# Split projection weights kept in DRAM by the first token group and loaded by the others

## The chip, the cores and the metric

One of the eight cores of a Trainium2 chip runs the whole kernel. Its time is device time in microseconds of one execution, from the start of the program to its end. An execution's profile shows the span from the first to the last instruction; the execution itself lasts a little longer than that span.

## The reference

The reference is one inference step of one layer of a streaming encoder, for a prompt of 2048 tokens and a sample of 32 tokens, each of width 1024, all in float32:

```python
z = rmsnorm(x, norm_mix_g) @ w_in                       # 1024 -> 2560: q, k, v and the RWKV inputs
a_out = window_attention(q, k, v, ...)                  # 8 heads, 2 KV heads, window of 2 chunks of 64, sinks
r_out, shift, S = rwkv7_mixer(zr, ...)                  # 8 heads of 64, a recurrence over the tokens
x = x + concat(a_out, r_out) @ w_out                    # 1024 -> 1024
x = x + memory_cross_attention(rmsnorm(x), mem_k, mem_v) # 4 heads of 128, 256 memory tokens, w_cq and w_co
x = x + square(relu(rmsnorm(x) @ w_up)) @ w_down        # 1024 -> 4096 -> 1024
y = rmsnorm(x, norm_final_g)
```

It returns the two outputs y, and the key, value, shift and recurrence states.

## The kernel before, in words

Features lie on the 128 partitions, tokens along the free dimension. The 2080 tokens are cut into four groups: `GROUPS` has 544 tokens in group 0 (the sample first) and 512 in each of groups 1, 2 and 3. A group is projected in two halves of 272 or 256 tokens.

**Products in three parts.** A float32 weight is split into a high part `w_h`, in the rounded format that TensorE multiplies fast, and a low part `w_l`, the rest. Activations are split in the same way into `xh` and `xl`. `mm3` multiplies `w_h` by `xh`, `w_h` by `xl` and `w_l` by `xh` into one PSUM tile (lines 234, 235 and 236). So 24 matmuls make one block of 128 output features for one half of a group.

**Where the weights are split.** `load_w` (line 257 issues the load) works in two halves of 512 columns. For each it loads a raw tile of 256 KB over the SP queue, rounds it to `w_h` with an activation on ScalarE (through `split`, line 66), and subtracts that from the raw tile to get `w_l` on POOL or VectorE (line 69). There are `RB = 2` raw tiles and `WB = 2` pairs of `w_h` and `w_l`, which all dense layers of the first stage share. A pair is 1024 columns of high and as many of low parts: 0.5 MB each.

**Dense layers.** `dense` goes through the units of a weight matrix, one `load_w` for each, and multiplies each unit by both halves of the group. The input projection has 20 units (`win`), the output projection 8 (`wout`), the query projection of the cross-attention 4 (`wcq`), its output projection 4 of two blocks each (`wco`), and the memory's keys and values 4 each. A unit is loaded and split again for every group: 4 x 20 for `win` and 4 x 8 for `wout`. Nearly all `w_l` of this stage are made on POOL; the first two units of group 0 on VectorE (`fast`).

**Evacuation.** `evac` scales a block out of PSUM into `zo` (three tiles) on VectorE, mixes neighbouring tokens for the RWKV part, and stores it to DRAM over SP. `ophase` adds the residual `xres`.

**The phases.** `Y` and `Z` project a group's RWKV and attention inputs (`zphase`), `R` is one RWKV tile of 128 tokens, `A` one attention tile, `O` the output projection (`ophase`), `C`, `X` and `D` the cross-attention. A string `PLAN` fixes the order in which they are traced; `Y0` comes first, `Z0` after it, then the memory phase `M` and the phases of groups 1 to 3 interleaved with the RWKV and attention tiles. The RWKV tiles are a chain: each needs the state of the one before. Inside a tile, a triangular solve sends a matrix through DRAM (`lscr`, `lt`), runs 15 steps of two short VectorE operations each (`prd`, `xt`), and sends the result through DRAM again (`xscr`, `td`). After all this the MLP runs for six blocks of 352 or 320 tokens (`ps_up`, `ps_dn`), with weights split in the same way.

**What sets the order on each engine.** The instructions are traced with priorities (`setp`), and a planner that simulates the engines' times orders all instructions of each engine and queue at compile time. On the chip, each engine and each queue then runs its own list strictly in that order, and an instruction that waits holds back everything behind it on the same engine or queue. Nearly all loads and stores are issued by SP, a few stores by ScalarE. Tiles with the same tag rotate through their buffers; a new tile waits until all users of the old one are done.

Of the kernel before, what the change touches and what calls it, by code (L numbers as in the profile page):

```python
# [10 lines left out]
F32 = mybir.dt.float32  # L11
F32R = mybir.dt.float32r
# [5 lines left out]
P = 128  # L18
# [4 lines left out]
KC = D // P  # L23
# [13 lines left out]
TCKW = dict(schedule_with_timeline_sim=True)  # L37
E1, E2, E3, E4, E6, E7, E8 = "GGGVGGV"
PSOL, PSER, RB, SNB = "s", "s", 2, 3
XB, WB, XS = 5, 2, 4  # L40
BKB, ABB, TMB = 2, 2, 2

PG = dict(mix=0, cross=8, mlp=16, fin=24, mem=32, mu=40, w0=54, a0=58, kk=62, ka=66,
# [7 lines left out]
def hymba_step_kernel(  # L51
# [9 lines left out]
    V, G, S, T, Q = nc.vector, nc.gpsimd, nc.scalar, nc.tensor, nc.sync  # L61
# [15 lines left out]
    dram = ctx.enter_context(tc.tile_pool(name="dram", bufs=1, space=DRAM))  # L77
# [170 lines left out]
    zp = stage1.enter_context(tc.tile_pool(name="zp", bufs=1))  # L248
# [3 lines left out]
    def load_w(pool, src, n=1024, bufs=3, tag="w", eng=None, rb=RB, raw=None):  # L252
        wh = pool.tile([P, n], F32R, tag=tag + "h", name="w_h", bufs=bufs)
        wl = pool.tile([P, n], F32R, tag=tag + "l", name="w_l", bufs=bufs)
        for i in range(0, n, 512):
            w = (raw or pool).tile([P, 512], F32, tag="wraw", name="w_raw", bufs=rb)
            Q.dma_start(w, src[:, i:i + 512])
            split(w, wh[:, i:i + 512], wl[:, i:i + 512], ENG[E7] if eng is G and i else eng)
        return wh, wl
# [36 lines left out]
            gsplit(xk(k), xh[a][:, b, 0:nb], xl[a][:, b, 0:nb], pc(gkey, k))  # L296
        return xh, xl, lambda: rms(zp, xk, nb, "zt", pe, 3)

    def dense(wsrc, units, xs, blks, evac, nk=KC, per=1, rs=None, fast=False):
        cols = nk * P  # L300
        if rs is None:
            rs = [None] * len(blks)
        for u in units:
            wh, wl = load_w(zp, wsrc[u], bufs=WB, eng=V if fast and u < units[0] + 2 else G)
            for j in range(per):
                ft = u * per + j
                for bi, (b0, nb) in enumerate(blks):
                    if callable(xs[bi]):
                        xs[bi] = xs[bi]()
                    xh, xl, r = xs[bi]  # L310
                    ps = pmm("ps_z")
                    mm3(ps[:, 0:nb], lambda k: wh[:, j * cols + k * P:j * cols + (k + 1) * P],
                        lambda k: wl[:, j * cols + k * P:j * cols + (k + 1) * P],
                        lambda k: xh[k // XS][:, k % XS, 0:nb], lambda k: xl[k // XS][:, k % XS, 0:nb], nk)
                    if rs[bi] is None and r is not None:
                        rs[bi] = r()
                    evac(ft, bi, b0, nb, ps, rs[bi])
# [3 lines left out]
    def zphase(g, units):  # L321
        lab(f"Z{g}.prep")
        o, n = GROUPS[g]
        blks = halves_of(g)
# [5 lines left out]
        xs, rs = zst[g]  # L330
# [29 lines left out]
                    V.tensor_copy(carry[:, f:f + 1], zms[f])  # L360
            Q.dma_start(zqkv[g][:, ft, b0:b0 + nb] if ft < 6 else zrw[g][:, ft - 6, b0:b0 + nb], zo[:, 0:nb])

        dense(win, units, xs, blks, evac, rs=rs, fast=(g == 0 and 0 not in units))
        if 0 in units:
            zouts(g)
        else:
# [40 lines left out]
    def ophase(g):  # L407
        lab(f"O{g}")
        o, n = GROUPS[g]
        blks = halves_of(g)  # L410
        xs = [prep(mscr[g][:, :, b0:b0 + nb], nb, None) for b0, nb in blks]

        def evac(m, bi, b0, nb, ps, r):
            xr = zp.tile([P, NH], F32, tag="zm", name="xres", bufs=3)
            Q.dma_start(xr[:, 0:nb], xT3[:, m, o + b0:o + b0 + nb])
            zo = zp.tile([P, NH], F32, tag="zo", name="zo2", bufs=3)
            tt(zo[:, 0:nb], ps[:, 0:nb], xr[:, 0:nb], ADD)
            Q.dma_start(x2scr[g][:, m, b0:b0 + nb], zo[:, 0:nb])

        dense(wout, range(8), xs, blks, evac)  # L420

    def cqphase(g):
        lab(f"C{g}")
# [477 lines left out]
    xs, hhs, hls, vrs = {}, {}, {}, {}  # L901
# [26 lines left out]
    for it in PLAN.split():  # L928
# [6 lines left out]
        elif k in "RA":  # L935
            g = it[1] if it[1] == "s" else int(it[1])
# [104 lines left out]
    for s_ in range(start[5] + 16):  # L1041
        up = []
        for i in range(2):
            u = (2 * s_ + i) % 3
# [127 lines left out]
```

## Time and profile before

| | |
|---|---|
| median of three runs (lowest, highest) | 3261.2 us (3257.07, 3262.8) |
| the profiled execution | 3264.61 us |
| its span | 3262.8 us |
| mean granted TensorE clock | 0.960 |
| busy: TensorE, VectorE, ScalarE, POOL | 93%, 58%, 38%, 31% of the span |
| moved by DMA | 328.95 MB, mean 101 GB/s |

A busy share is the time in which an engine has an instruction under way, over the span; matmuls are pipelined, so a busy TensorE is not always at its peak rate. Of two operations with the same name, one belongs to a line of the kernel (L66 is an activation, L69 and L72 two forms of elementwise operation, all in helpers), so tile names tell them apart: `w_l<-w_raw,w_h` writes `w_l` and reads `w_raw` and `w_h`. "Idle before" is the time in which the engine stood still ahead of an instruction, put down to what ended it. The chain that ended last is followed back from the last instruction: at each step to what released it.

### The profile page before, as it was taken

How to read it: one execution, taken by the hardware profiler on the slowest of the kernel's cores; microseconds unless marked ns; L12 is line 12 of the kernel's file. 1: busy time of each engine (PE TensorE's matmuls, PEld its weight loads, DVE VectorE, ACT ScalarE, POOL GpSimd, SP SyncE). 2: the span in 40 equal slices, each digit the busy share in tenths (PEclk: the TensorE clock that was granted, in tenths of full speed). 3: DMA queues.
4: the chain of work that ended last, by engine and by line, in shares of the span. 5: the costliest groups of instructions: out<-in, count | busy, mean ns of one | idle time of the engine just before them, and what ended most of it. 6: DMA issues, size and time to landing. Idle time of an engine off the chain costs nothing.

```text
span 3262.8 us, 64716 instructions
## 1 busy us (share of the span) xinstructions
PE 3037.4 (93%) x25605; PEld 2850.0 (87%) x25605; DVE 1896.0 (58%) x4482; ACT 1247.0 (38%) x2824; POOL 1012.4 (31%) x1017
## 2 busy tenths in 40 slices
PE   8989888998879988898978999999999999999998
PEld 7877776877768977778978999999999999999998
DVE  4588777887777567853334544444445644444446
ACT  5355454444455444445443322222224322222223
POOL 3443354323354343425554410111013511011111
PEclk9989888999989999999989999999999999999999
DMA  5443343334344454446765211111113111111112
GB/s 167 134 115 108 104 130 108 108 96 122 109 122 123 135 150 120 130 129 195 242 214 178 68 51 41 46 46 52 40 46 115 66 44 52 40 52 52 46 46 91
DMA packets 336752, 328.95 MB, mean 101 GB/s; under 512 B 82320, under 2 KB 256064, under 8 KB 336448
## 3 DMA queue, kind: packets, MB, share of 16 engines
q1 hardware_dynamic: 306640, 311.83, 31.0%
q10 hardware_dynamic: 29808, 12.98, 1.6%
q8 instruction: 201, 3.29, 0.4%
q14 instruction: 103, 0.84, 0.1%
HBM read 252.59 MB, written 72.39 MB: 100 GB/s over the span
## 4 chain that ended last, share of the span: by engine, by line
PE 53%; DMA 8%; DVE 7%; ACT 3%; POOL 2%; issue 2%; SPq 1%; DVEq 0%; ACTq 0%; POOLq 0%
PE ps_up L236 7%; PE ps_dn L1002 7%; PE ps_dn L1004 7%; PE ps_dn L1003 7%; PE ps_up L234 7%; PE ps_up L235 7%; PE ps_z L234 2%; PE ps_z L236 2%; PE ps_z L235 2%; DMA xb<-x2scr 2%; DMA lt<-lscr 1%; ACT xh L66 1%; DVE z L69 1%; DVE prd L69 1%; DVE xt L69 1%
## 5 line engine op out<-in xcount | busy, mean ns | idle before, releaser
L234 PE MATMUL ps_z<-xh,w_h 128*128 128x256 f32 (+1 forms) x2368 | 722.8, 305 | 98.3 <-DVE zo L69 41.1
L236 PE MATMUL ps_z<-xh,w_l 128*128 128x256 f32 (+1 forms) x2368 | 715.0, 302 | 0.8 <-POOL w_l L69 0.8
L235 PE MATMUL ps_z<-xl,w_h 128*128 128x256 f32 (+1 forms) x2368 | 714.0, 302 | 1.4 <-DVE xl L72 0.8
L66 ACT ACTIVATE w_h<-w_raw 128x512 fp32r<-128x512 f32 x576 | 344.5, 626 | 777.7 <-PE ps_up L235 258.5
L69 DVE TENSOR_TENSOR x<-ps_dn,x 128x352 f32<-128x352 f32 (+1 forms) x768 | 389.6, 516 | 365.0 <-PE ps_dn L1004 364.5
L234 PEld LDWEIGHTS ps_z<-xh,w_h 128*128 128x128 f32 x2368 | 478.0, 202 | 124.1 <-DVE zo L69 34.2
L69 POOL TENSOR_TENSOR w_l<-w_raw,w_h 128x512 fp32r<-128x512 f32 x300 | 394.9, 1332 | 580.6 <-ACT w_h L66 481.0
L69 POOL TENSOR_TENSOR rl<-rl 128x352 f32<-128x352 f32 (+1 forms) x192 | 161.1, 840 | 1138.4 <-ACT uh L66 1136.4
L1002 PE MATMUL ps_dn<-uh,w_h 128*128 128x352 f32 (+1 forms) x1536 | 492.9, 321 | 4.2 <-DVE x L69 3.1
L236 PE MATMUL ps_up<-fh,w_l 128*128 128x352 f32 (+1 forms) x1536 | 495.4, 323 | 1.2 <-DVE w_l L69 1.2
L1003 PE MATMUL ps_dn<-ul,w_h 128*128 128x352 f32 (+1 forms) x1536 | 491.1, 320 | 5.0 <-DVE ul L69 5.0
L234 PE MATMUL ps_up<-fh,w_h 128*128 128x352 f32 (+1 forms) x1536 | 493.2, 321 | 0.5 <-DVE zo L69 0.5
L235 PEld LDWEIGHTS ps_z<-xl,w_h 128*128 128x128 f32 x2368 | 478.3, 202 | 15.9 <-issue 9.6
L236 PEld LDWEIGHTS ps_z<-xh,w_l 128*128 128x128 f32 x2368 | 478.0, 202 | 15.2 <-issue 10.4
L235 PE MATMUL ps_up<-fl,w_h 128*128 128x352 f32 (+1 forms) x1536 | 491.1, 320 | 0.1
L1004 PE MATMUL ps_dn<-uh,w_l 128*128 128x352 f32 (+1 forms) x1536 | 490.8, 320 | 0.0
L69 DVE TENSOR_TENSOR w_l<-w_raw,w_h 128x512 fp32r<-128x512 f32 x276 | 197.7, 735 | 222.0 <-ACT w_h L66 221.5
L1003 PEld LDWEIGHTS ps_dn<-ul,w_h 128*128 128x128 f32 x1536 | 289.9, 189 | 5.6 <-DVE ul L69 5.3
L1002 PEld LDWEIGHTS ps_dn<-uh,w_h 128*128 128x128 f32 x1536 | 288.6, 188 | 6.5 <-DVE x L69 3.0
L236 PEld LDWEIGHTS ps_up<-fh,w_l 128*128 128x128 f32 x1536 | 288.4, 188 | 1.7 <-DVE w_l L69 1.5
L1004 PEld LDWEIGHTS ps_dn<-uh,w_l 128*128 128x128 f32 x1536 | 289.2, 188 | 0.2
L234 PEld LDWEIGHTS ps_up<-fh,w_h 128*128 128x128 f32 x1536 | 288.3, 188 | 1.3 <-DVE zo L69 0.7
(245 smaller groups left out, 4478.5 us busy)
## 6 DMA issues: line engine op xcount, KB each, us to landing
w_raw<-in_win SPq DMA_DIRECT2D x160, 256.0 KB, 2.9
w_raw<-in_wup SPq DMA_DIRECT2D x136, 256.0 KB, 2.6
w_raw<-in_wdn SPq DMA_DIRECT2D x136, 256.0 KB, 2.6
w_raw<-in_wout SPq DMA_DIRECT2D x64, 256.0 KB, 3.2
zrw<-zo SPq DMA_DIRECT2D x84, 128.0 KB, 2.1
lt<-lscr SPq DMA_DIRECT2D x34, 244.0 KB, 3.8
zin<-zrw SPq DMA_DIRECT2D x16, 512.0 KB, 3.8
w_raw<-in_wcq SPq DMA_DIRECT2D x32, 256.0 KB, 3.4
```

Of the source, the lines that this page charges most:

```text
L66: S.activation(out, in_, func, **kw)
L69: (eng or V).tensor_tensor(out, a, b, op=op)
L234: T.matmul(ps, lhsT=a, rhs=c, start=(k == 0), stop=False)
L235: T.matmul(ps, lhsT=a, rhs=d, start=False, stop=False)
L236: T.matmul(ps, lhsT=b, rhs=c, start=False, stop=(k == nk - 1))
L1002: T.matmul(ps[:, 0:n], lhsT=wh[:, ms], rhs=us[i][0], start=(i == 0), stop=False)
L1003: T.matmul(ps[:, 0:n], lhsT=wh[:, ms], rhs=us[i][1], start=False, stop=False)
L1004: T.matmul(ps[:, 0:n], lhsT=wl[:, ms], rhs=us[i][0], start=False, stop=(i == 1))
```

## The change

`stage_w` takes the place of `load_w` in `dense`. For `win` and `wout` (`keep` is "in" or "out"), group 0 loads and splits each unit as before and then stores the finished `w_h` and `w_l` to two DRAM tiles, over SP. When groups 1, 2 and 3 come to the same unit, they load `w_h` and `w_l` from there, over SP, each in one transfer of 512 KB, straight into a pair of buffers; no raw tile, no activation and no subtraction is needed. `wcq`, `wco` and the memory's weights are split in place as before. The pairs of buffers become three (`WB = 3`) for all dense layers of the first stage.

```diff
--- before.py
+++ after.py
@@ -37,7 +37,7 @@
 TCKW = dict(schedule_with_timeline_sim=True)
 E1, E2, E3, E4, E6, E7, E8 = "GGGVGGV"
 PSOL, PSER, RB, SNB = "s", "s", 2, 3
-XB, WB, XS = 5, 2, 4
+XB, WB, XS = 5, 3, 4
 BKB, ABB, TMB = 2, 2, 2
 
 PG = dict(mix=0, cross=8, mlp=16, fin=24, mem=32, mu=40, w0=54, a0=58, kk=62, ka=66,
@@ -296,12 +296,31 @@
             gsplit(xk(k), xh[a][:, b, 0:nb], xl[a][:, b, 0:nb], pc(gkey, k))
         return xh, xl, lambda: rms(zp, xk, nb, "zt", pe, 3)
 
-    def dense(wsrc, units, xs, blks, evac, nk=KC, per=1, rs=None, fast=False):
+    wsaved = {}
+
+    def stage_w(wsrc, u, keep, fast):
+        key = (keep, u)
+        if key in wsaved:
+            dh, dl = wsaved[key]
+            wh = zp.tile([P, 1024], F32R, tag="wh", name="w_h", bufs=WB)
+            wl = zp.tile([P, 1024], F32R, tag="wl", name="w_l", bufs=WB)
+            Q.dma_start(wh.bitcast(F32), dh)
+            Q.dma_start(wl.bitcast(F32), dl)
+            return wh, wl
+        wh, wl = load_w(zp, wsrc[u], bufs=WB, eng=V if fast else G)
+        if keep is not None:
+            dh, dl = [dram.tile([P, 1024], F32, name=f"w{keep}{u}{c}") for c in "hl"]
+            Q.dma_start(dh, wh.bitcast(F32))
+            Q.dma_start(dl, wl.bitcast(F32))
+            wsaved[key] = (dh, dl)
+        return wh, wl
+
+    def dense(wsrc, units, xs, blks, evac, nk=KC, per=1, rs=None, fast=False, keep=None):
         cols = nk * P
         if rs is None:
             rs = [None] * len(blks)
         for u in units:
-            wh, wl = load_w(zp, wsrc[u], bufs=WB, eng=V if fast and u < units[0] + 2 else G)
+            wh, wl = stage_w(wsrc, u, keep, fast and u < units[0] + 2)
             for j in range(per):
                 ft = u * per + j
                 for bi, (b0, nb) in enumerate(blks):
@@ -360,7 +379,7 @@
                     V.tensor_copy(carry[:, f:f + 1], zms[f])
             Q.dma_start(zqkv[g][:, ft, b0:b0 + nb] if ft < 6 else zrw[g][:, ft - 6, b0:b0 + nb], zo[:, 0:nb])
 
-        dense(win, units, xs, blks, evac, rs=rs, fast=(g == 0 and 0 not in units))
+        dense(win, units, xs, blks, evac, rs=rs, fast=(g == 0 and 0 not in units), keep="in")
         if 0 in units:
             zouts(g)
         else:
@@ -417,7 +436,7 @@
             tt(zo[:, 0:nb], ps[:, 0:nb], xr[:, 0:nb], ADD)
             Q.dma_start(x2scr[g][:, m, b0:b0 + nb], zo[:, 0:nb])
 
-        dense(wout, range(8), xs, blks, evac)
+        dense(wout, range(8), xs, blks, evac, keep="out")
 
     def cqphase(g):
         lab(f"C{g}")
```

## Rows read from the trace of the kernel before

**Rows 1.** windows: length; PE, PEld, DVE, ACT, POOL busy; clock, DMA share, GB/s

```profile
0.00:118.00 118.00, 104.79 (x745) 98.05 (x746) 56.41 (x182) 57.49 (x128) 44.51 (x48) 1.00 0.50 161
118.00:170.00 52.00, 45.76 (x340) 42.67 (x338) 32.02 (x53) 20.12 (x39) 25.57 (x21) 0.93 0.44 134
170.00:1500.00 1330.00, 1177.22 (x13478) 1015.06 (x13478) 984.85 (x2699) 660.73 (x1590) 531.63 (x498) 0.92 0.42 120
1500.00:1770.00 270.00, 236.09 (x1793) 228.61 (x1793) 84.79 (x191) 123.92 (x294) 132.10 (x139) 0.93 0.70 224
1770.00:3262.00 1492.00, 1473.56 (x9257) 1465.66 (x9255) 737.90 (x1360) 384.76 (x774) 278.55 (x311) 1.00 0.17 55
```

**Rows 2.** the page's chain that ended last, share of the span by engine

```profile
PE 53%; DMA 8%; DVE 7%; ACT 3%; POOL 2%; issue 2%; SPq 1%; DVEq 0%; ACTq 0%; POOLq 0%
```

**Rows 3.** the chain from 800 to 1770 us, share of that stretch by line

```profile
by line: PE ps_z L234 7.7%; PE ps_z L236 7.4%; PE ps_z L235 7.4%; issue 5.6%; DMA xb<-x2scr 5.1%; DMA lt<-lscr 3.1%; ACT xh L66 2.4%; DVE z L69 2.3%; DVE prd L69 2.2%; DVE xt L69 2.2%; DMA lscr<-ab 2.1%; PE xpo L498 2.0%; POOL w_l L69 2.0%;
```

**Rows 4.** waits from 170 to 1770 us, TensorE: us, times, longest

```profile
PE ps_z L236 <- POOL w_l L69: 0.8, 2, 0.6
```

**Rows 5.** waits from 170 to 1770 us, ScalarE

```profile
ACT w_h L66 <- PE ps_z L235: 77.2, 38, 7.1
```

**Rows 6.** waits from 170 to 1770 us, the SP queue

```profile
SPq L257 <- POOL w_l L69: 203.7, 126, 9.0
```

**Rows 7.** POOL's group, 170-1770 us: count, busy, mean ns, idle before

```profile
L69 POOL TENSOR_TENSOR w_l<-w_raw,w_h 128x512 fp32r<-128x512 f32 x260 | 342.1, 1332 | 497.0 <-ACT w_h L66 398.4 <-PE ps_z L236 34.1 <-PE ptm L225 13.3
```

**Rows 8.** the same view, 800 to 1770 us, ScalarE, POOL and VectorE

```profile
L66 ACT ACTIVATE w_h<-w_raw 128x512 fp32r<-128x512 f32 x170 | 100.2, 625 | 130.5 <-PE ps_z L235 64.3 <-DMA w_raw<-in_wco 26.3 <-DMA w_raw<-in_wout 12.2
...
L69 POOL TENSOR_TENSOR w_l<-w_raw,w_h 128x512 fp32r<-128x512 f32 x165 | 215.2, 1319 | 279.4 <-ACT w_h L66 241.6 <-PE ptm L225 13.3 <-PE pq L225 7.8
...
L69 DVE TENSOR_TENSOR prd<-xt,lt 128x30 f32<-128x30 f32 (+10 forms) x120 | 29.5, 246 | 24.4 <-DMA lt<-lscr 21.7
...
L69 DVE TENSOR_TENSOR xt<-xt,prd 128x30 f32<-128x30 f32 (+10 forms) x120 | 28.7, 239 | 3.0
```

**Rows 9.** the same view, 0 to 1800 us, VectorE operations with two SBUF inputs

```profile
L69 DVE TENSOR_TENSOR xt<-xt,prd 128x30 f32<-128x30 f32 (+10 forms) x255 | 62.7, 246 | 6.2
...
L69 DVE TENSOR_TENSOR prd<-xt,lt 128x30 f32<-128x30 f32 (+10 forms) x255 | 61.8, 242 | 45.3 <-DMA lt<-lscr 39.6
...
L573 DVE TENSOR_TENSOR_SCAN cs<-cst,wa 128x128 f32<-128x128 f32 x68 | 40.9, 656 | 1.8 <-ACT wa L66 1.8
```

**Rows 10.** those three by tile: count, duration ns min/median/max

```profile
L69 DVE TENSOR_TENSOR xt<-xt,prd x255: 151/185/1342, 180.7 to 1423.6; 128x30 f32<-128x30 f32 x25, 128x14 f32<-128x14 f32 x16, 128x24 f32<-128x24 f32 x16, 128x15 f32<-128x15 f32 x9
...
L69 DVE TENSOR_TENSOR prd<-xt,lt x255: 120/184/1301, 180.5 to 1422.9; 128x30 f32<-128x30 f32 x25, 128x14 f32<-128x14 f32 x16, 128x24 f32<-128x24 f32 x16, 128x15 f32<-128x15 f32 x9
...
L573 DVE TENSOR_TENSOR_SCAN cs<-cst,wa x68: 390/406/1521, 129.0 to 1364.6; 128x128 f32<-128x128 f32 x68
```

**Rows 11.** timeline from 746 us: start, us, engine, operation

```profile
746.60 0.19 DVE L69 TENSOR_TENSOR prd<-xt,lt 128x30 f32<-128x30 f32 x1
...
746.88 2.51 POOL L69 TENSOR_TENSOR w_l<-w_raw,w_h 128x512 fp32r<-128x512 f32 x2 [2.64 <-ACT w_h L66]
...
747.05 1.14 DVE L69 TENSOR_TENSOR prd<-xt,lt 128x24 f32<-128x24 f32 x1
...
748.22 1.21 DVE L69 TENSOR_TENSOR xt<-xt,prd 128x24 f32<-128x24 f32 x1
```

**Rows 12.** raw weights, landing time: 40 to 118 us, then 1500 to 1650

```profile
DMA to landing us min/median/max: 2.4/3.0/4.5
...
DMA to landing us min/median/max: 2.4/3.4/8.9
```

**Rows 13.** main DMA queue: packets, MB, share; 40-118 us, then 1500-1650

```profile
q1 hardware_dynamic: 8779, 10.58, 42.2%
...
q1 hardware_dynamic: 28630, 31.87, 67.4%
```

**Rows 14.** TensorE from 60 to 80 us, columns as in rows 1

```profile
60.00:80.00 20.00, 20.00 (x161) 20.00 (x160) 10.25 (x32) 8.38 (x18) 9.18 (x8) 1.00 0.39 128
```

## The prediction

> **What bounds the kernel now.** I read the busy times by stretch first. Before 1770 us the kernel projects, runs the RWKV and attention tiles and cross-attends; after that it is the MLP. There TensorE is busy 1473.56 of 1492 us at granted clock 1.00 [rows 1]: nothing to win, and nothing of the change lies in it. From 170 to 1770 us, where groups 1 to 3 are projected, TensorE is idle 152.8 + 33.9 = 186.7 us, VectorE busy 74% up to 1500 us, ScalarE 50%, POOL 40%, the DMA engines 42%, and 70% from 1500 to 1770 us [rows 1]. No engine is full, so the order of dependent steps sets the time. The chain that ended last shows that: half of the span on TensorE (nearly all of it MLP), then DMA 8%, VectorE 7%, ScalarE 3%, POOL 2% [rows 2]; from 800 to 1770 us (its first recorded part) it runs through projections, loads of `xb`, and the solve of the RWKV tile (`lt`, `prd`, `xt`) [rows 3]. The reader is to see that it hops among engines, so work matters by what it delays, not by its engine's share.
>
> Does TensorE wait for weights? Hardly: 0.8 us for `w_l` on POOL [rows 4]. The conversion hurts others: ScalarE, in order, stands 77.2 us before a `w_h` whose buffer TensorE still reads [rows 5], and SP 203.7 us before raw loads until POOL frees a raw tile [rows 6].
>
> **The change, part by part.** Units in groups 1 to 3: 3 x (20 + 8) = 84, each two halves: 168 halves out of the 260 that POOL converts from 170 us on [rows 7].
>
> *Removed on POOL.* 168 x 1.332 = 224 us of 663.7 us busy [rows 1, 7]. What was on the path: `POOL w_l` is 2.0% of 970 us = 19.4 us of the chain, for 165 conversions [rows 3, 8]. So 0.118 us each, and for 168: 20 us; I lower it to 19, since the copies left are the cross-attention's, which stand late, where the chain is. Ends: 0 (another path takes over) and 224 x 19.4/215.2 x 2 = 40 (the unrecorded first part as sensitive again).
>
> *Removed on ScalarE.* 168 x 0.625 = 105 us [rows 8]. ScalarE has 3% of the span on the chain, 98 us, in 784.7 us of work from 170 to 1770 us [rows 1, 2]: 12.5%, so 13 us; I take 10, as `w_h` is a step that can often wait. Ends 0 and 77, the whole wait for TensorE.
>
> *VectorE.* It loses no instruction, but some get shorter. A `prd` takes 0.19 us; one that begins inside a pair of `w_l` (2.51 us on POOL from 746.88) takes 1.14, and the `xt` behind it 1.21: they end just as the first and second copy end [rows 11]. Means stand above medians by this: `xt` 246 against 185, `prd` 242 against 184, `cs` 656 against 406 ns: 255 x 61 + 255 x 58 + 68 x 250 = 47 us [rows 9, 10]. If all of it were `w_l`, removing 168 of 260 frees 31 us; if only POOL's share of time in `w_l` (342.1 of 663.7) counts, 16 us [rows 1, 7]. Of the solve, 4.4% of 970 = 42.7 us lies on the chain, of 58.2 us busy: 73% [rows 3, 8]. So 12 to 23 us; other VectorE operations with two inputs come on top, so 20. Ends 0 and 47.
>
> The Trainium skill (SBUF — State Buffer, "Who interferes with whom") says that VectorE's second port pair is GpSimd's and is locked for a whole instruction, so that the loser blocks. The trace agrees: 1.14 us instead of 0.19 [rows 11]. By that rule alone all 168 copies could stop hiding VectorE time, and the term would stand at its upper end.
>
> *Added: stores.* 28 units x 2 x 0.524 MB = 29.4 MB, 56 issues on SP, each behind the conversion it stores. Behind a waiting store on SP stand the z stores (`zo` has three tiles) and the next raw loads. From 40 to 118 us TensorE does 161 matmuls in 20 us without a pause [rows 14], so a unit of 48 takes 5.96 us. The queue moved 10.58 MB at 42.2% of 78 us [rows 13], a full rate of 321 GB/s. A unit there will move 0.52 load + 1.05 stores + 0.28 z = 1.85 MB, 5.8 us of 5.96: nearly full. A raw tile's cycle is landing 3.0 + 0.63 + 1.33 = 5.0 us [rows 7, 8, 12], 1.0 us spare. A load behind one 0.524 MB store lands 1.6 us later: 0.6 us lost per unit, 7.6 us over the 12 units after the first two; behind both, 2.3 us and 27 us; behind none, 0. I take 6, as loads and stores alternate and the first copy hides in spare time. Z0 and O0 space their units wider; nothing there.
>
> *Added: twice the load.* 84 x 0.524 = 44 MB more, 137 us at 321 GB/s, 8.6% of 1600 us. Landing rose from 3.0 to 3.4 us when the queue's share rose from 42.2% to 67.4% [rows 12, 13]: 8.6 points give 0.14 us, 4.6%. On all DMA of the chain, 8% = 261 us [rows 2], that is 12 us. Ends 0 (prefetched loads delay nobody) and 40 (bursts in 1500 to 1770 us, already at 70%, fill up).
>
> *Moved waits; a third buffer.* The load now waits on SP until TensorE frees a pair; behind it stand the solve's `lt` and `td` loads and z stores. In exchange 168 of 260 raw loads lose their wait for POOL: 203.7 x 0.65 = 132 us of SP time [rows 6, 7]. ScalarE's 77.2 us [rows 5] moves to SP at worst, and three pairs make it rarer. Zero, ends -20 and +20. The 8 KB more per partition shift what lies behind the projection pool, so that first MLP weights may come later: TensorE is idle only 18.4 us of the whole MLP [rows 1]; zero, ends -6 and +6. The planner orders all engines anew; no row shows that, and I leave it to the range.
>
> *Sum.* -19 - 10 - 20 + 6 + 12 = -31 us. A shortened chain makes the next path late, and what is left to win is the 186.7 us of idle TensorE, in which every path ends; so two thirds, -21 us. The profiled execution has 3264.6 us around its span of 3262.8: 3243.6. It lies 3.4 us over the median of the runs, 3261.2: 3240 us.
>
> **The rivals.**
>
> *A, more.* The planner fills TensorE's idle time denser, as three pairs also serve the cross-attention units (`POOL w_l` late in the chain) and VectorE runs freer. A third of 186.7 us less 10 for the DMA: -52, 3209 us. For: VectorE at 74%; against: 34 of the 186.7 us lie in 1500 to 1770 us at DMA 70% [rows 1].
>
> *B, nothing.* The conversions stand in gaps: TensorE waits 0.8 us for them [rows 4], and the chain turns to `xb` loads (5.1% [rows 3]). Gains of 12 against 18 of costs and back: 3261 us, within 6.5.
>
> *C, slower: the store traffic of Y0.* From 97% of the DMA rate on, each load waits for both stores: +27 us, in the one stretch where TensorE never pauses, while groups 1 to 3 give half of their net, -8: 3280 us. It decides once raw weights land later than 5.96 - 0.63 - 1.33 = 4.0 us. Against: at 67.4% they still landed in 3.4 [rows 12, 13]. The Trainium skill (DMA: Bandwidth & Descriptors, "Queues, rings and completion order") says that each DMA engine takes descriptors in ring order; no row here has a store of this size ahead of a load.
>
> *D, not as told.* The loads could miss their gain if the planner puts them too late to be prefetched; TensorE would then wait on `w_h` loads. It counts with C.
>
> **How the numbers follow.** Forecast 0.46 (3224 to 3254), A 0.20, B 0.14, C and D 0.20. This measurement tells apart about 0.2%, 6.5 us. Faster: 0.46 + 0.20 = 0.66; same 0.14; slower 0.20. The range runs from 3195 (A's better half is left out, 0.08) to 3282 (C's worse end, 0.09 left out).
>
> **What would show it.** Right: `w_l` on POOL falls from 300 to 132; `prd` and `xt` means approach 185 ns, except in Y0, Z0 and the memory phase; TensorE's idle time from 170 to 1770 us falls by some 20 us, with Y0 about 6 us longer; landing of `lt` and `xb` rises little. Wrong: raw weights in Y0 landing over 4 us with pauses in TensorE there (C); TensorE waiting on the loaded `w_h` or SP on TensorE for long (D); POOL and VectorE relieved, but TensorE's idle time unchanged (B).

## The result and the profile after

The changed kernel took 3202.31 us (median of four runs, 3193.85 to 3208.01) beside 3260.57 us for the kernel before in the same comparison: a ratio of 0.9819, 95% interval 0.9805 to 0.9833. That is 58 us faster; 21 were forecast. The sign and the range held, the size did not: it is nearly three times the forecast, and close to rival A's 52.

The page's busy times come first: before, and then after. Each engine has its busy time and the number of its instructions.

```profile
PE 3037.4 (93%) x25605; PEld 2850.0 (87%) x25605; DVE 1896.0 (58%) x4482; ACT 1247.0 (38%) x2824; POOL 1012.4 (31%) x1017
```

```profile
PE 3012.1 (94%) x25605; PEld 2826.1 (88%) x25605; DVE 1803.7 (56%) x4482; ACT 1157.8 (36%) x2656; POOL 788.5 (25%) x849
```

VectorE runs the same 4482 instructions in 1896.0 - 1803.7 = 92.3 us less. That line alone says that something stopped holding its instructions up. POOL lost 168 instructions and 223.9 us, ScalarE 168 and 89.2 us, as the code has it.

By stretch (length; TensorE, weight loads, VectorE, ScalarE, POOL busy; granted clock, DMA share, GB/s), to be read against [rows 1]; the MLP now begins at 1709 us:

```profile
0.00:118.00 118.00, 99.82 (x705) 92.86 (x706) 54.67 (x175) 54.66 (x122) 40.36 (x45) 1.00 0.81 277
118.00:170.00 52.00, 43.90 (x317) 40.76 (x316) 28.58 (x49) 17.70 (x32) 24.21 (x20) 0.97 0.82 273
170.00:1500.00 1330.00, 1212.23 (x13955) 1050.53 (x13956) 913.95 (x2753) 614.83 (x1522) 363.03 (x383) 0.95 0.55 168
1500.00:1709.00 209.00, 180.84 (x1376) 175.45 (x1376) 62.52 (x146) 82.31 (x198) 76.73 (x85) 0.93 0.72 238
1709.00:3206.00 1497.00, 1475.27 (x9261) 1466.52 (x9260) 743.96 (x1360) 388.26 (x782) 284.14 (x317) 0.99 0.17 55
```

From 170 us to the MLP TensorE is idle 117.8 + 28.2 = 146.0 us instead of 186.7, and in the first 170 us 26.3 instead of 19.4. Over the whole span its idle time falls by 31 us; the other 25 us are its busy time (3037.4 to 3012.1 for the same 25605 matmuls), with the granted clock of 170 to 1500 us up from 0.92 to 0.95 of 2.4 GHz. The MLP takes 1497 us where it took 1492.8: the first four loads of its raw weights are issued 38 to 19 us ahead of it, where the kernel before issued them 211 to 195 us ahead, and 4 us go back. With two pairs in the changed kernel (below) it takes 1492.7 us again, so this is the third pair's part.

The solve's `prd` runs once in each of 15 steps of 17 RWKV tiles; first and last start give the pace of the whole chain of tiles. Against [rows 10]:

```profile
L69 DVE TENSOR_TENSOR prd<-xt,lt x255: 140/183/1289, 188.4 to 1352.2; 128x30 f32<-128x30 f32 x25, 128x14 f32<-128x14 f32 x16, 128x24 f32<-128x24 f32 x16, 128x15 f32<-128x15 f32 x9
```

It begins 8 us later (188.4 against 180.5) and ends 71 us earlier (1352.2 against 1422.9). So the first group cost 8 us, the stretch with RWKV tiles gave 79, and from there to the MLP 10 us are lost again (357 us against 347).

POOL's copies fall from 300 to 132 over the whole span: the 168 are gone. From 170 to 1709 us, against [rows 7], 96 are left, of the memory, output group 0 and the cross-attention.

```profile
L69 POOL TENSOR_TENSOR w_l<-w_raw,w_h 128x512 fp32r<-128x512 f32 x96 | 124.1, 1307 | 174.1 <-ACT w_h L66 141.7 <-DMA td<-xscr 25.7 <-DMA w_raw<-in_wout 3.4
```

VectorE's groups (count, busy, mean ns, idle before), against [rows 9]:

```profile
L69 DVE TENSOR_TENSOR xt<-xt,prd 128x30 f32<-128x30 f32 (+10 forms) x255 | 51.8, 203 | 5.5
...
L69 DVE TENSOR_TENSOR prd<-xt,lt 128x30 f32<-128x30 f32 (+10 forms) x255 | 53.6, 210 | 53.2 <-DMA lt<-lscr 48.1
...
L592 DVE TENSOR_TENSOR_SCAN cs<-cst,wa 128x128 f32<-128x128 f32 x68 | 29.7, 490 | 5.9 <-ACT wa L66 5.9
```

The means fell from 246, 242 and 656 to 203, 210 and 490 ns, and the three groups together from 165.4 to 135.1 us: 30.3 of VectorE's 92.3 us. The other 62 lie elsewhere. Three of the larger ones, before and then after (to 1800 us):

```profile
L72 DVE SCALAR_TENSOR_TENSOR zo<-zo,omu,zm 128x256 f32<-128x256 f32 (+3 forms) x126 | 81.7, 648 | 51.2 <-ACT zm L66 49.1
...
L69 DVE TENSOR_TENSOR z<-kk,pp 64x256 f32<-64x256 f32 x66 | 68.6, 1076 | 0.2
...
L853 DVE TENSOR_SCALAR sc<-sc,sm 128x256 f32<-128x256 f32 (+2 forms) x136 | 57.5, 476 | 0.6
```

```profile
L72 DVE SCALAR_TENSOR_TENSOR zo<-zo,omu,zm 128x256 f32<-128x256 f32 (+3 forms) x126 | 71.8, 573 | 62.2 <-ACT zm L66 60.8
...
L69 DVE TENSOR_TENSOR z<-kk,pp 64x256 f32<-64x256 f32 x66 | 59.6, 940 | 0.3
...
L872 DVE TENSOR_SCALAR sc<-sc,sm 128x256 f32<-128x256 f32 (+2 forms) x136 | 47.3, 400 | 0.6
```

What was added, against [rows 12 to 14]: landing of raw weights and the main DMA queue from 40 to 118 us, and TensorE from 60 to 80 us.

```profile
DMA to landing us min/median/max: 2.5/3.7/6.6
```

```profile
q1 hardware_dynamic: 11517, 21.60, 79.1%
```

```profile
60.00:80.00 20.00, 18.38 (x146) 18.19 (x145) 9.07 (x31) 7.02 (x16) 7.66 (x6) 1.00 0.83 288
```

The queue went from 42.2% to 79.1%, landing from 3.0 to 3.7 us, and TensorE does 146 matmuls in 20 us where it did 161: Y0 now has pauses.

The waits on SP and on ScalarE (us in total, times, longest), against [rows 5, 6]:

```profile
SPq L307 <- PE ps_z L236: 116.0, 50, 8.7
...
SPq L257 <- POOL w_l L69: 56.0, 45, 5.3
```

```profile
ACT w_h L66 <- PE ps_z L235: 44.8, 15, 7.4
```

SP's 203.7 us before raw tiles became 56.0, with 116.0 us before loads that wait for TensorE in their place; ScalarE's 77.2 us fell to 44.8. The chain from 800 to 1709 us, against [rows 3], names `POOL w_l`, `prd` and `xt` no longer among the entries shown, and the projection's three matmul lines are 29.7% of it instead of 22.5%:

```profile
by line: PE ps_z L234 10.1%; PE ps_z L235 9.9%; PE ps_z L236 9.7%; DMA xb<-mscr 3.1%; DMA xres<-x2scr 2.9%; issue 2.9%; PE xpo L517 2.5%; DMA xb<-x2scr 2.3%; DVE z L69 2.2%; DMA lt<-lscr 2.2%; DMA xscr<-xt 1.9%; DMA lscr<-ab 1.8%; PE xq L49
```

### The profile page after: what moved, and what is told of

It reads as the page before. It is cut to its first block, busy times and chain, and to the rows that moved or that the text cites. A ratio compares the mean times of both kernels' runs of the same rounds, so it can differ in the third digit from the quotient of the medians.

```text
span 3206.2 us, 64370 instructions
## 1 busy us (share of the span) xinstructions
PE 3012.1 (94%) x25605; PEld 2826.1 (88%) x25605; DVE 1803.7 (56%) x4482; ACT 1157.8 (36%) x2656; POOL 788.5 (25%) x849
## 4 chain that ended last, share of the span: by engine, by line
PE 61%; DVE 11%; DMA 9%; ACT 2%; issue 2%; POOL 1%; SPq 1%; ACTq 0%; DVEq 0%; POOLq 0%
PE ps_up L236 7%; PE ps_dn L1021 7%; PE ps_up L234 7%; PE ps_dn L1023 7%; PE ps_up L235 7%; PE ps_dn L1022 7%; PE ps_z L234 4%; PE ps_z L235 3%; PE ps_z L236 3%; DVE z L69 1%; DMA lt<-lscr 1%; DMA lscr<-ab 1%; DMA xscr<-xt 1%; PE pA L225 1%; DMA xb<-mscr 1%
## 5 line engine op out<-in xcount | busy, mean ns | idle before, releaser
L234 PE MATMUL ps_z<-xh,w_h 128*128 128x256 f32 (+1 forms) x2368 | 712.9, 301 | 72.9 <-DVE zo L69 35.8
L236 PE MATMUL ps_z<-xh,w_l 128*128 128x256 f32 (+1 forms) x2368 | 699.4, 296 | 0.6 <-POOL w_l L69 0.6
L234 PEld LDWEIGHTS ps_z<-xh,w_h 128*128 128x128 f32 x2368 | 466.1, 197 | 98.6 <-DVE zo L69 36.4
L66 ACT ACTIVATE w_h<-w_raw 128x512 fp32r<-128x512 f32 x408 | 247.1, 627 | 703.5 <-PE ps_up L235 258.5
L235 PEld LDWEIGHTS ps_z<-xl,w_h 128*128 128x128 f32 x2368 | 466.0, 197 | 31.5 <-issue 10.4
L236 PEld LDWEIGHTS ps_z<-xh,w_l 128*128 128x128 f32 x2368 | 466.2, 197 | 13.1 <-issue 8.7
L235 PEld LDWEIGHTS ps_up<-fl,w_h 128*128 128x128 f32 x1536 | 288.5, 188 | 3.0 <-DVE fl L72 2.7
```

The lines of the kernel that those rows point to most:

```text
L66: S.activation(out, in_, func, **kw)
L234: T.matmul(ps, lhsT=a, rhs=c, start=(k == 0), stop=False)
L235: T.matmul(ps, lhsT=a, rhs=d, start=False, stop=False)
L236: T.matmul(ps, lhsT=b, rhs=c, start=False, stop=(k == nk - 1))
```

## The experiments

Ratios are to the kernel before in the same comparison, with 95% intervals; the change itself is 0.9819. A difference in ratio of 0.001 is 3.3 us. Theories: **P**, POOL's copies (by holding up VectorE, **L**, or by their time in POOL's queue, **Q**, or by weights waiting for them, **W**); **A**, ScalarE's activations; **B**, the third pair of buffers.

**Three pairs alone**

```diff
-XB, WB, XS = 5, 2, 4
+XB, WB, XS = 5, 3, 4
```

> The kernel before with three pairs of weight buffers instead of two; nothing is stored or loaded instead of split. Theory P (the relief of POOL carries the gain, by the VectorE operations that it held up and by the steps queued behind the copies on POOL): within 8 us of before, 3252 to 3268. Theory B (the third pair of buffers carries it: ScalarE no longer waits for TensorE, loads run further ahead): 3240 or less, a third of the 58 us or more. Theory A (ScalarE's relief carries it): 3240 to 3255, as only its wait for a free pair gets shorter.

Measured 3246.2 us, 0.9940 (0.9919 to 0.9960): 20 us faster. That is more than P allows, at the edge of what B asks (3240, a third of the 58 us), and inside A's range. But ScalarE's wait for a free pair, from which A expected it, only fell from 77.2 to 63.0 us, so what made the 20 us stays open.

**Two pairs in the changed kernel**

```diff
-XB, WB, XS = 5, 3, 4
+XB, WB, XS = 5, 2, 4
```

> The changed kernel with two pairs of weight buffers instead of three. Theory P: within 10 us of the changed kernel, 3195 to 3213. Theory B: 3225 to 3260, most of the gain gone. Theory A: 3200 to 3215.

Measured 3204.47 us, 0.9810 (0.9786 to 0.9835): the same as the change, as P and A expected. Theory B falls: the whole gain is there without the third pair. What three pairs give the old kernel, the changed one does not need.

**Low parts back on POOL**

```diff
-            Q.dma_start(wl.bitcast(F32), dl)
+            for i in range(0, 1024, 512):
+                w = zp.tile([P, 512], F32, tag="wraw", name="w_raw", bufs=RB)
+                Q.dma_start(w, wsrc[u][:, i:i + 512])
+                tt(wl[:, i:i + 512], w, wh.bitcast(F32)[:, i:i + 512], SUB, G)
```

> The changed kernel, but in groups 1 to 3 only the high part is loaded; the raw halves are loaded too and POOL makes the low part from them, so the bytes loaded are those of the change and POOL has its 168 copies back, while ScalarE stays relieved. Theory P: most of the gain gone, 3235 to 3260. Theory A: most of it stays, 3200 to 3215.

Measured 3315.35 us, 1.0152 (1.0127 to 1.0178): 109 us over the change, and slower than the kernel before. More than P expected. In this kernel SP stands before raw loads until POOL frees a raw tile (L310 is the new load), in line with all other transfers, and the bytes are the change's:

```profile
SPq L310 <- POOL w_l L69: 198.0, 109, 9.7
```

The kernel before has such a wait too (241.3 us over the same stretch, to 1770 us), so the wait doesn't explain why this run is slower than that kernel, which loads fewer bytes; the cause stays open. The run mixes POOL's time with waits, bytes and order and can size none of them.

**High parts back on ScalarE**

```diff
-            Q.dma_start(wh.bitcast(F32), dh)
+            for i in range(0, 1024, 512):
+                w = zp.tile([P, 512], F32, tag="wraw", name="w_raw", bufs=RB)
+                Q.dma_start(w, wsrc[u][:, i:i + 512])
+                act(wh[:, i:i + 512], w)
```

> The changed kernel, but in groups 1 to 3 only the low part is loaded; the raw halves are loaded too and ScalarE makes the high part from them: ScalarE has its 168 activations back, POOL stays relieved, the bytes are those of the change. Theory P: most of the gain stays, 3200 to 3220. Theory A: 3230 to 3255.

Measured 3228.91 us, 0.9881 (0.9857 to 0.9905): 20 us of the 58 gone, 38 left, between P's range and A's. ScalarE has a part, with the raw loads that come with it.

**Idle copies on POOL**

```diff
+    scrap = const.tile([P, 512], F32, name="scrap")
...
             Q.dma_start(wl.bitcast(F32), dl)
+            for i in range(0, 1024, 512):
+                tt(scrap, bias.rearrange("p a b -> p (a b)")[:, i:i + 512], bias.rearrange("p a b -> p (a b)")[:, 1024 + i:1536 + i], SUB, G)
```

> The changed kernel (0.982 of the kernel before), with 168 subtractions of 128x512 put back on POOL in groups 1 to 3, two beside each pair of loads: they read a table and write scrap that nobody reads, so no weight waits for them. Theory L (POOL's reading copies hold up VectorE operations with two inputs, and that is the larger part): VectorE's prd and xt means go back to about 240 ns and the time to 3232 to 3255 (0.991 to 0.998). Theory Q (steps queued behind the copies on POOL): the same loss here and with memsets. Theory W (weights and raw tiles waiting for the copies, not the copies' own time): 3200 to 3212.

Measured 3283.64 us, 1.0067 (1.0041 to 1.0094): 81 us lost, with not one weight waiting. W falls. It is also more than L expected, with `xt` and `prd` at 266 and 267 ns. But the planner put these copies, which wait for nothing, into the first 500 us (from 24 to 42 in each 100 us, where the kernel before has 14 to 22), so they stand denser than the real ones.

**Idle memsets on POOL**

```diff
+            for i in range(2):
+                for n in (512, 512, 128):
+                    G.memset(scrap[:, 0:n], 0.0)
```

> The changed kernel with memsets of scrap on POOL in the same places, about 1.4 us for each of the 168 halves, as long as the subtractions but with no input to read. Theory L: prd and xt stay near 210 ns, time within 10 us of the changed kernel, 3195 to 3215. Theory Q: 3225 to 3255, like the idle subtractions. Theory W: 3200 to 3212.

Measured 3214.0 us, 0.9850 (0.9823 to 0.9877): 10 us over the change, with intervals that overlap, bunched in the first 400 us in the same way. For L, with the place and the length (207 us more on POOL than the change, where the idle copies brought 223) not quite equal. The next two were made for that.

**Copies before the loads** and **memsets before the loads**: POOL writes into the fresh low tile what the load then overwrites, so that the operations stand near the units' places and the loads wait for both kinds alike (SP waits 50.6 us for copies and 53.7 for memsets ahead of the low part's load). The places come close without being equal: from 400 to 500 us there are 2 copies and 6 groups of three memsets, from 700 to 800 us 13 and 6.

```diff
+            for i in range(0, 1024, 512):
+                tt(wl[:, i:i + 512], bias.rearrange("p a b -> p (a b)")[:, i:i + 512], bias.rearrange("p a b -> p (a b)")[:, 1024 + i:1536 + i], SUB, G)
             Q.dma_start(wh.bitcast(F32), dh)
             Q.dma_start(wl.bitcast(F32), dl)
```

> The changed kernel; in groups 1 to 3 POOL writes two subtractions of 128x512 into a fresh low tile before its load overwrites it, so the 168 copies stand where the units are, not bunched early as the idle ones were. Theory L (POOL's reading copies hold up VectorE): 40 to 90 us over the changed kernel, 0.994 to 1.010 of the kernel before, with prd and xt means about 240 ns, and far more than the memsets in the same place. Theory Q (POOL's time and the delay of the loads behind it): the same loss as with memsets.

```diff
+            for i in range(0, 1024, 512):
+                for j in range(3):
+                    G.memset(wl.bitcast(F32)[:, i:i + 512], 0.0)
             Q.dma_start(wh.bitcast(F32), dh)
             Q.dma_start(wl.bitcast(F32), dl)
```

> The same with memsets in place of the subtractions (three of 0.43 us for each half, 1.3 us), which have no input to read; the loads wait for them in the same way. Theory L: at most 20 us over the changed kernel, 0.982 to 0.988, prd and xt near 205 ns. Theory Q: as much as with the subtractions.

Measured with copies 3263.47 us, 1.0000 (0.9983 to 1.0018): the whole gain is gone. With memsets 3205.21 us, 0.9832 (0.9801 to 0.9864): all of it is there. The pages, copies first:

```profile
PE 3043.6 (93%) x25605; PEld 2847.5 (87%) x25605; DVE 1899.2 (58%) x4482; ACT 1158.6 (36%) x2656; POOL 1013.5 (31%) x1017
```

```profile
PE 3017.2 (94%) x25605; PEld 2827.0 (88%) x25605; DVE 1843.2 (57%) x4482; ACT 1158.8 (36%) x2656; POOL 1030.8 (32%) x1353
```

POOL is busy longer with memsets (1030.8 us against 1013.5), VectorE 56.0 us less (1843.2 against 1899.2), and the time is 58 us less (55 by the ratios). Their groups on POOL and VectorE, copies first:

```profile
L69 POOL TENSOR_TENSOR w_l<-bias 128x512 fp32r<-128x512 f32 x168 | 226.3, 1368 | 335.1 <-PE ps_z L236 189.5 <-issue 135.8 <-DMA win5l<-w_l 6.5
...
L69 DVE TENSOR_TENSOR xt<-xt,prd 128x30 f32<-128x30 f32 (+10 forms) x255 | 73.4, 288 | 5.7
...
L69 DVE TENSOR_TENSOR prd<-xt,lt 128x30 f32<-128x30 f32 (+10 forms) x255 | 68.7, 269 | 51.8 <-DMA lt<-lscr 46.7
...
L874 DVE TENSOR_SCALAR sc<-sc,sm 128x256 f32<-128x256 f32 (+2 forms) x136 | 52.0, 438 | 0.7
```

```profile
L309 POOL MEMSET w_l<- 128x512 f32 x504 | 248.9, 537 | 276.3 <-PE ps_z L236 248.2 <-issue 25.1 <-ACT ab L66 1.0
...
L875 DVE TENSOR_SCALAR sc<-sc,sm 128x256 f32<-128x256 f32 (+2 forms) x136 | 64.0, 523 | 0.6
...
L69 DVE TENSOR_TENSOR xt<-xt,prd 128x30 f32<-128x30 f32 (+10 forms) x255 | 57.0, 224 | 5.3
...
L69 DVE TENSOR_TENSOR prd<-xt,lt 128x30 f32<-128x30 f32 (+10 forms) x255 | 56.4, 221 | 48.2 <-DMA lt<-lscr 43.0
```

Beside copies, `xt` and `prd` (two inputs in SBUF) take 288 and 269 ns in the mean; beside memsets 224 and 221. (The change has 203 and 210, the changed kernel with two pairs 234 and 220 in the same time, so differences of 20 ns or so can be order.) The two groups are 28.7 of the 56.0 us. Their steps from the first tile to the last, copies first:

```profile
L69 DVE TENSOR_TENSOR prd<-xt,lt x255: 109/185/1332, 190.1 to 1432.4; 128x30 f32<-128x30 f32 x25, 128x14 f32<-128x14 f32 x16, 128x24 f32<-128x24 f32 x16, 128x15 f32<-128x15 f32 x9
```

```profile
L69 DVE TENSOR_TENSOR prd<-xt,lt x255: 139/183/1206, 188.9 to 1365.7; 128x30 f32<-128x30 f32 x25, 128x14 f32<-128x14 f32 x16, 128x24 f32<-128x24 f32 x16, 128x15 f32<-128x15 f32 x9
```

With copies the chain of RWKV tiles takes 1242.3 us, as in the kernel before (1242.4); with memsets 1176.8, near the change's 1163.8. That is where the copies' loss lies.

Memsets hold up another kind: `sc`, an operation with one large input, takes 523 ns, beside copies 438, and in the changed kernel 400 (its line is above). So memsets also stall VectorE (39.5 us more busy than the change), but the time grows by only 4 us by the ratios, less than the noise, while copies stall the chain of tiles. Q falls, L stands.

**Idle copies on ScalarE**

```diff
+            for i in range(0, 1024, 512):
+                act(scrap, bias.rearrange("p a b -> p (a b)")[:, i:i + 512])
```

> The changed kernel with 168 activations of 128x512 (0.63 us each, 105 us) put back on ScalarE in groups 1 to 3, writing scrap that nobody reads and waiting for nothing. The prediction's term for ScalarE says +10 us, 3212. If ScalarE's time itself made the 27 us that the run with the high parts on ScalarE lost: 3225 to 3235. If that loss came from waits for raw loads and free buffers: 3200 to 3210.

Measured 3209.67 us, 0.9848 (0.9817 to 0.9878): 9 us by the ratios, near the term's 10, but the interval holds the change's 0.9819, and the planner bunched them in the first 300 us. By these values ScalarE's time is about half of the 20 us above, and the rest came with raw loads and buffers; the noise leaves anything from 0 to 19 us.

**Idle loads**

```diff
+            for i in range(0, 1024, 512):
+                w = zp.tile([P, 512], F32, tag="wraw", name="w_idle", bufs=RB)
+                Q.dma_start(w, wsrc[u][:, i:i + 512])
```

> The changed kernel with the raw halves loaded as well in groups 1 to 3 (168 loads of 256 KB, 44 MB, over SP) and read by nobody: as many bytes again as the change added to the loads of these groups. The prediction's term says +12 us, 3214. If more traffic is what made the run with the low parts on POOL slower than the kernel before: 3240 or more. If loads that nobody waits for are free: within 6 us, 3196 to 3208.

Measured 3249.51 us, 0.9955 (0.9938 to 0.9973): 45 us. SP waits for the landing of an earlier idle load before it issues the next but one into the same tile, with everything behind it:

```profile
SPq L311 <- DMA w_idle<-in_win: 99.0, 74, 6.6
...
SPq L311 <- DMA w_idle<-in_wout: 37.8, 32, 3.7
```

137 us of SP's time. But SP waits less elsewhere in turn (53.4 us for TensorE ahead of the loaded high parts, where the change has 116.0), so this is again a mixture, of bytes, waits and order. The next run asks what the bytes alone are worth.

**High parts only**: groups 1 to 3 load the high part alone and multiply it in the low part's place too.

```diff
-            wl = zp.tile([P, 1024], F32R, tag="wl", name="w_l", bufs=WB)
...
             Q.dma_start(wh.bitcast(F32), dh)
-            Q.dma_start(wl.bitcast(F32), dl)
-            return wh, wl
+            return wh, wh
```

> The changed kernel, but groups 1 to 3 load only the high part and multiply it in the low part's place too: the bytes loaded there are those of the kernel before (44 MB fewer than the change), the matmuls are the same. By the prediction's term for twice the load: 12 us under the changed kernel, 0.978. By the 45 us that 44 MB of idle loads cost: 30 us or more under it, 0.973 or less. If those idle loads cost by their waits on SP and not by bytes: within 8 us of it.

Measured 3193.21 us, 0.9789 (0.9761 to 0.9818): 10 us for 44 MB and 84 issues, 12 by the term. The interval overlaps the change's, and the run's solve begins at 183.1 us instead of 188.4, though group 0 does the same work: some of the 10 us is order. Either way 44 MB fewer give far less than 45 us. That the rest of the idle loads' 45 us is their waits on SP is argued from this and not shown.

**One store**: only the first unit is stored, and groups 1 to 3 load that one in the place of every unit.

```diff
+    wone = []
...
+            if wone:
+                wsaved[key] = wone[0]
+                return wh, wl
             dh, dl = [dram.tile([P, 1024], F32, name=f"w{keep}{u}{c}") for c in "hl"]
...
+            wone.append(wsaved[key])
```

> The changed kernel, but only the first unit is stored and all units of groups 1 to 3 load that one: 27 of the 28 units' stores are gone, the loads stay. By the prediction's term for the stores: 6 us under the changed kernel, 0.980, with Y0 back to its length of before (118 us, where the change has 125) and Z0 too. If the first group's 8 us carry through: 0.979 to 0.980; if they are hidden later: 0.982.

Measured 3186.69 us, 0.9777 (0.9749 to 0.9805): 14 us. Its first two stretches (columns as above):

```profile
0.00:118.00 118.00, 103.46 (x739) 96.66 (x740) 59.40 (x181) 58.36 (x130) 45.62 (x50) 1.00 0.54 174
118.00:170.00 52.00, 45.87 (x343) 42.46 (x341) 31.81 (x56) 16.87 (x34) 17.93 (x16) 0.93 0.56 174
```

TensorE is busy 103.46 of the first 118 us, against 104.79 before and 99.82 in the change, and the DMA share is 0.54 against 0.81 (0.50 before). Its solve begins at 179.8 us, as in the kernel before (180.5), where the change begins at 188.4; the rest of the 14 us lies behind that. With the same stores in group 0, though, the solve begins anywhere from 183.1 (high parts only) to 194.1 us (two pairs), so order has a part in this too. Whether loading one unit again and again is cheaper than loading 28 was not tried.

**Low part first**: stores and loads of the low part ahead of the high part's, the same work.

```diff
-            Q.dma_start(wh.bitcast(F32), dh)
             Q.dma_start(wl.bitcast(F32), dl)
+            Q.dma_start(wh.bitcast(F32), dh)
```

(and the two stores in the same way)

> The changed kernel with the low part stored and loaded ahead of the high part: the same work, ordered anew by the planner. It shows how far a new order alone moves the time: if planning is worth little, within 10 us of the changed kernel, 0.979 to 0.985 of the kernel before; if the third pair's 0.6% in the kernel before was such luck, as much either way here, 0.975 or 0.988.

Measured 3212.66 us, 0.9850 (0.9830 to 0.9870): 10 us slower by nothing but order. A difference of 10 us between these kernels therefore shows no cause by itself; the 20 us of three pairs are twice that.

**Output projection only** and **input projection only**

```diff
-        dense(win, units, xs, blks, evac, rs=rs, fast=(g == 0 and 0 not in units), keep="in")
+        dense(win, units, xs, blks, evac, rs=rs, fast=(g == 0 and 0 not in units))
```

> The changed kernel with only the output projection's weights kept (48 of the 168 copies gone, 120 back, three pairs). If the gain goes with the number of reading copies taken from POOL, 0.33 us for each from the run with copies before the loads: 16 us, less 3 for bytes and up to 4 for stores: 9 to 13 us from that, on top of 0 to 20 for the third pair, 3227 to 3251 (0.990 to 0.997). If VectorE's stalls cost only beside the RWKV tiles of the early groups: 0.994 to 1.000.

```diff
-        dense(wout, range(8), xs, blks, evac, keep="out")
+        dense(wout, range(8), xs, blks, evac)
```

> The changed kernel with only the input projection's weights kept: 120 copies gone, the 48 of the output projection back on POOL. If a copy costs where the RWKV and attention tiles run beside it and little late: the gain of the change stays, 0.979 to 0.984, with VectorE's busy time down by some 70 of the 92 us. If it goes with the number of copies: 0.986 to 0.989.

Measured: output projection only (48 copies gone) 3247.9 us, 0.9962 (0.9949 to 0.9975), 12 us; input projection only (120 gone) 3226.67 us, 0.9876 (0.9856 to 0.9895), 40 us. By count, the 58 would part into 17 and 41. VectorE's busy time fell by 26.1 and 62.5 us (the pages below against 1896.0), by count 26.4 and 65.9 of 92.3:

```profile
PE 3023.8 (93%) x25605; PEld 2835.4 (87%) x25605; DVE 1869.9 (58%) x4482; ACT 1226.1 (38%) x2776; POOL 950.6 (29%) x969
```

```profile
PE 3026.8 (94%) x25605; PEld 2838.5 (88%) x25605; DVE 1833.5 (57%) x4482; ACT 1182.4 (37%) x2704; POOL 851.7 (26%) x897
```

So VectorE's time goes with the number of copies for these two matrices, and the expectation of "place" fails for them. The kernel's time does so only as long as it is counted from the kernel before. Both runs have three pairs, and three pairs alone gave the old kernel 0.9940: counted from there, keeping the output projection gave nothing by itself (0.9962), although its chain of tiles is shorter (1212 us against 1235), and 19 us beside the input projection (0.9876 to 0.9819). So these two runs don't give a price for one copy.

**Keep the cross-attention's weights too**, and **the same with the sums of squares on TensorE**

```diff
-        dense(wcq, range(4), xs, blks, evac)
+        dense(wcq, range(4), xs, blks, evac, keep="cq")
...
-        dense(wco, range(4), xs, blks, evac, 4, 2)
+        dense(wco, range(4), xs, blks, evac, 4, 2, keep="co")
```

> The changed kernel with the cross-attention's query and output weights kept in the same way (48 more copies off POOL, 132 to 84, and 12.6 MB more loaded in groups 1 to 3, 8 units more stored). By 0.33 us for each copy, less 3 for bytes and 4 for stores: 9 us under the changed kernel, 0.979. If the late stretch from 1500 us is bound by its DMA (share 0.7 before): no gain or a loss, 0.982 or more.

```diff
-                return prep(xT3[:, :, o + b0:o + b0 + nb], nb, "mix", pe=(g == 0), alt=(g == 0 and b0 > 0))
+                return prep(xT3[:, :, o + b0:o + b0 + nb], nb, "mix", pe=True, alt=(g == 0 and b0 > 0))
...
-        xs = [prep(x2scr[g][:, :, b0:b0 + nb], nb, "cross") for b0, nb in blks]
+        xs = [prep(x2scr[g][:, :, b0:b0 + nb], nb, "cross", pe=True) for b0, nb in blks]
```

> The same, and the sums of squares of the input and cross-attention norms go through TensorE instead of POOL in groups 1 to 3 too (98 additions of 0.8 us with two inputs gone from POOL, 112 short matmuls more). If POOL's reading time is what counts, 78 us of it at 0.25 us of gain for each us (55 for 224): 19 us under the run that keeps all, 0.973. If TensorE's added work takes it back: the same as that run.

Measured 3205.5 us, 0.9829 (0.9809 to 0.9849), and 3224.71 us, 0.9896 (0.9873 to 0.9918). Neither beats the change. In the first, 48 more copies gone took only 12.8 us more from VectorE's busy time, and the late stretch now has a DMA share of 0.84 where the change has 0.72:

```profile
PE 3015.3 (94%) x25605; PEld 2826.6 (88%) x25605; DVE 1790.9 (56%) x4482; ACT 1135.2 (35%) x2608; POOL 727.5 (23%) x801
```

```profile
1500.00:1707.00 207.00, 177.84 (x1355) 171.70 (x1355) 58.12 (x144) 65.22 (x166) 33.34 (x52) 0.93 0.84 280
```

VectorE is busy 58 of 207 us there: copies find little to hold up. Which of the two, the little to win or the bytes, ate the 9 us is not separated. In the second, 98 additions are gone from POOL and 196 matmuls have come to TensorE (the expectation had 112):

```profile
PE 3043.8 (95%) x25801; PEld 2843.3 (88%) x25801; DVE 1796.2 (56%) x4482; ACT 1133.4 (35%) x2608; POOL 648.3 (20%) x703
```

TensorE is busy 28.5 us longer than in the first, POOL 79.2 us less, and VectorE no less (1796.2 us against 1790.9): these additions read two inputs as well, and taking them away freed no VectorE time. So a microsecond on POOL has no fixed price, and the 0.25 us of gain for each in the expectation did not hold. The run is 19 us slower than the first.

**Input projection only, stores from ScalarE's queue**

```diff
-            Q.dma_start(dh, wh.bitcast(F32))
-            Q.dma_start(dl, wl.bitcast(F32))
+            S.dma_start(dh, wh.bitcast(F32))
+            S.dma_start(dl, wl.bitcast(F32))
```

> The same with the stores issued by ScalarE instead of SP, so that no z store or raw load of group 0 stands behind a store that waits for its conversion. If the 14 us of the stores are waits on SP: 8 to 12 us under the run with the input projection alone. If they are bytes on the DMA engines: no difference. If ScalarE, now waiting for POOL ahead of each low part's store, holds up its own work: slower.

Measured 3243.14 us, 0.9934 (0.9917 to 0.9952): 19 us slower than from SP, and the solve begins at 203.7 us instead of 186.3. ScalarE's list is the worse place for these stores here; whether SP's waits were part of the 14 us stays open.

## Why the prediction was wrong, step by step

**The step that failed is the term for VectorE**: "So 12 to 23 us; other VectorE operations with two inputs come on top, so 20. Ends 0 and 47." The mechanism was right, the size was not: with POOL's time, the places and the loads' waits nearly alike, copies cost 1.0000 - 0.9832 = 0.0168, 55 us, more than memsets, above the term's upper end. What made it small are the other operations: the sentence names them and then gives them nothing, as 20 lies inside the 12 to 23 of `xt`, `prd` and `cs`. Those three lost 30.3 us of busy time, just what the term's first reading had for them (31); VectorE as a whole lost 92.3, so two thirds of what there was to free (`zo`, `z`, with one large input `sc`, and others) were put at nothing. The share of the path was not too low: of the 95.5 us that copies put on VectorE over the change, 58, or 61%, came out as time, where the term took 73%. The prediction's own bound for the case that all 168 copies stop hiding VectorE time, 47 us, came nearer.

**POOL, 19 us**: the term counted POOL's own time. With memsets POOL is busy longer than with copies, and the time stays within the change's noise (0.9801 to 0.9864 against 0.9805 to 0.9833): 4 us by the ratios, 15 at most. Why the steps that named `POOL w_l` on the chain gave no more, no run shows. Together the two terms were 39 us and measured some 59 (the run with copies against the change), about 55 of them by what the copies read.

**Two thirds of the sum**: wrong. The terms' full sum, -31, would have given 3230. The idle time that was left to win was no bound: 31 us of the gain are TensorE's idle time, and 25 us are matmuls that took less time, with the granted clock up from 0.92 to 0.95, which the working did not have at all.

**ScalarE, 10 us**: 9 us by idle activations, 20 us with the raw loads; not contradicted, but the 9 us are within the noise.

**Stores, 6 us**: near for Y0, 7 us (TensorE's 161 matmuls in 20 us became 146), though order moves that by several us. Landing rose to 3.7 us, under the 4.0 us from which rival C decides, though the queue's share nearly doubled. All stores together cost 14 us by the run with one store; if that holds, "Z0 and O0 space their units wider; nothing there" was too good. The 321 GB/s taken as the full rate was too low: 21.60 MB at 79.1% of 78 us are 350 GB/s.

**Twice the load, 12 us**: 10 us, not contradicted, but order and noise are as large.

**Moved waits and the third buffer, 0**: for the buffer right in the changed kernel (two pairs do as well), though the third pair alone is worth 20 us to the old one. The moved waits have no run of their own. SP does wait on TensorE for long, 116.0 us, which the prediction gave as a sign of rival D, but TensorE shows no wait for a `w_h` or `w_l` loaded from DRAM. The MLP's later first weights cost 4 us, inside the 6.

**Rival A, 52 us**, came near in the number, in part by luck. It gave the gain to TensorE's idle time, 62 of 186.7 us, and to three pairs; the idle time fell by 40.7 us, and the third pair gave the changed kernel nothing. The freer VectorE that it also named is what the runs show.

Adding up what the runs gave: -55 for copies, -9 to -20 for ScalarE, +14 for stores, +10 for bytes, -40 to -51 beside a measured -58, with some 10 us of order in each. Only the copies' part stands clear of that. The Trainium skill (SBUF — State Buffer, "SBUF: two separate sides") says which operations collide: VectorE's with two SBUF inputs "only against a GpSimd op that reads SBUF", others in a two-port mode against any GpSimd operation. The two runs agree to the kind: copies lengthen `xt` and `prd` (288 and 269 ns against 224 and 221), memsets lengthen `sc` (523 against 438); in which mode `sc` runs, no view shows. The prediction used the rule to find three groups that stall, and did not ask which other groups do.

## What to carry to other kernels

Where VectorE works through chains of short operations, price work on POOL by what it holds up on VectorE, and over all of VectorE's groups, not a few: the three that were counted carried 30 of 92 us. Afterwards, VectorE's busy time over the same instruction count shows the whole. To tell an engine's time from what its reads do, put operations of the same length without inputs in the same places. A load's price is not only in its bytes: leaving out 44 MB of needed loads gave 10 us, and adding 44 MB of idle ones, which waited for their tiles on SP, cost 45.

## What was not expected

POOL's memsets, which read nothing, raised VectorE's busy time by 39.5 us over the change without a measurable loss of time, while copies raised it by 95.5 us and lost all 58: what a stalled microsecond costs depends on the operation it falls on. And the order alone moved the time by 10 us when two transfers of equal size changed places.
